# One more pair of k-tiles through sums in every second unit of the down product, and weight parts in whole chunks

## Chip, core and metric

The kernel runs on one core of one Trainium2 chip. The metric is the device time of one execution in microseconds. The core has a matrix engine (PE, with its weight loads shown as PEld), a vector engine (DVE), a scalar engine (ACT), a general engine (POOL) and a queue engine (SP) that issues most of the transfers. Each engine works through its own list of instructions.

## What is computed

Two layers of a decoder on 256 tokens of width 2048, all in float32. Each layer is a mixer and then a squared-ReLU MLP of width 8192. The parts that matter here:

```python
def channel_mlp(h, w_up, w_down):
    a = jax.nn.relu(h @ w_up)
    return (a * a) @ w_down
...
    for layer in range(DEPTH):
        ...
        h = rms_norm(x, ffn_norm[layer])
        x = x + channel_mlp(h, w_up[layer], w_down[layer])
```

`h @ w_up` is the up product (2048 to 8192), `(a * a) @ w_down` the down product (8192 to 2048).

## The kernel before

**Parts.** Every float32 operand of the big products is split into a high part (a copy on ACT into the reduced type `float32r`) and a low part (what is left, a subtraction on DVE). A product of two tiles is then three matmuls: high by high, high by low, low by high. Weights are streamed from memory and split as they come: a chunk is four k-tiles of 128 rows by 512 columns (1 MB), in one of three buffers `raw`. Its parts go to the pools `whi` and `wlo`. Before the change a buffer there holds two k-tiles (128x1024), and each pool has six of them; `load_chunk` (L57) makes two copies and two subtractions a chunk.

**Units.** In the up product and the mixers' products, `unit` and `unit_t` run over four chunks. In the products that end a mixer and in the down product, `wide` (L146) takes two column blocks of 512 and eight places; a place is a pair of k-tiles for both column blocks. It keeps four PSUM tiles `C[t][q]` (c00, c01, c10, c11: token half t, column block q), which ACT first fills with x (L151) and which DVE adds into x at the end (L217). A plain place makes eight products of three matmuls (24). A place in `sums` treats the 2x2 blocks (token halves by k-tiles, k-tiles by column blocks) with seven products (21 matmuls): sums of activations come ready from `combine` (tiles `combs`), sums of weights are made on DVE in the `raw` buffer (L175 to L178). Four of the seven results (1, 5, 7, 6) gather in PSUM tiles p1, p5, p7, p6 of their own. They are combined into s1, u2, u3 and w3 after the last place with sums (L197 to L201), at place 6.

**The down product.** `mlp` makes the up product in 16 blocks `up(j)` of 512 columns and the down product in four parts s. For each s, five blocks of `up` (four in the last) come first, then two units of `wide`: the first unit (`jw` = 0, output columns 0 to 1023) and the second unit (`jw` = 1, the rest). Both have sums at places 0, 2 and 4 of eight. So there are eight pairs of units in the two layers. At the end of layer 0, blocks of the next layer's input are turned (transposed on PE) from a list `pending`, one at place 6 and one at place 7 of the following unit, then one per chunk.

**Order.** A scheduler of the library orders the instructions of each engine when the program is built; every engine then takes its list in order and waits on semaphores. So instructions of several places can be interleaved, and the order changes with the code. The numbers behind tile names in the listings below are those of single buffers; they differ between the two programs.

Of the kernel before, what the change touches and what calls it, by code (L numbers as in the profile page):

```python
# [9 lines left out]
F32 = mybir.dt.float32  # L10
F32R = mybir.dt.float32r
# [5 lines left out]
P = 128  # L17
# [3 lines left out]
NB = 512  # L21
# [11 lines left out]
def trunk_kernel(ctx: ExitStack, tc, x, xT, vecs, sgu_gain, wsT, w_in, w_mix, w_qkv, w_ao, w_up, w_dn, out):  # L33
# [5 lines left out]
    parts = pool("parts", 6)  # L39
# [18 lines left out]
    def load_chunk(src, first=False):  # L58
# [3 lines left out]
        got = []  # L62
        for h in range(2):
            hi = parts.tile([P, 2, NB], F32R, name="whi")
            lo = parts.tile([P, 2, NB], F32R, name="wlo")
            for a, b in ((0, 1), (1, 2)) if first else ((0, 2),):
                w = raw[:, 2 * h + a:2 * h + b]
                nc.scalar.activation(hi[:, a:b], w, AF.Copy)  # L68
                nc.vector.tensor_tensor(lo[:, a:b], w, hi[:, a:b].bitcast(F32), ALU.subtract)  # L69
            got += [(hi[:, 0], lo[:, 0]), (hi[:, 1], lo[:, 1])]  # L70
# [50 lines left out]
    def combine(src):  # L121
# [8 lines left out]
        both = sums_of.tile([P, 2, 4, P], F32R, name="combs")  # L130
# [4 lines left out]
    def split_weights(w):  # L135

        n = w.shape[1]
        hi = parts.tile([P, 2, NB], F32R, name="whi")
        lo = parts.tile([P, 2, NB], F32R, name="wlo")
        nc.scalar.activation(hi[:, :n], w, AF.Copy)  # L140
        nc.vector.tensor_tensor(lo[:, :n], w, hi[:, :n].bitcast(F32), ALU.subtract)  # L141
        return hi, lo

    def wide(steps, src, x_of, sums=(0, 2, 4), last=False, behind=()):
# [14 lines left out]
        for n, (at, pair, i, comb) in enumerate(steps):  # L159
# [8 lines left out]
            cut = lambda both, q: tuple(w[:, q] for w in both)  # L168
            if n in sums:
# [3 lines left out]
                b11 = split_weights(left[:, 0:1])  # L173
                b2 = split_weights(raw[:, :, 1])
                nc.vector.tensor_tensor(left[:, 0], left[:, 0], right[:, 0], ALU.add)  # L175
                nc.vector.tensor_tensor(right[:, 0], right[:, 0], right[:, 1], ALU.add)  # L176
                nc.vector.tensor_tensor(right[:, 1], left[:, 0], right[:, 1], ALU.add)
                nc.vector.tensor_tensor(left[:, 1], right[:, 1], left[:, 1], ALU.add)  # L178
                t13 = split_weights(raw[:, :, 0])
                t42 = split_weights(raw[:, :, 1])  # L180
                if first:
                    mixed = {m: psum.tile([P, NB], F32, name=f"p{m}", tag="tp") for m in (1, 5, 7, 6)}
                for m in (1, 2, 3, 5, 7, 6, 4):
                    held, streamed = {
                        1: (a(0, 0), cut(b11, 0)), 2: (a(1, 0), cut(b2, 0)), 3: (s(3), cut(b2, 1)),
                        4: (a(1, 1), cut(t42, 0)), 5: (s(0), cut(t13, 0)), 6: (s(1), cut(t42, 1)),
                        7: (s(2), cut(t13, 1))}[m]
# [4 lines left out]
            else:  # L192
# [17 lines left out]
                for t, q, k in turns:  # L210
                    product(C[t][q], a(k, t), cut(both[k], q), False, n == 7 and k == 1)
# [465 lines left out]
```

## Time and profile before

| | |
|---|---|
| median of 3 runs | 2094.29 us (2094.15 to 2095.1) |
| the profiled execution | 2094.96 us, span 2093.2 us |
| PE busy | 2084.9 us, 100% of the span, 10300 matmuls |
| DVE busy | 1561.3 us, 75% |
| ACT busy | 1168.8 us, 56% |
| transfers | 403.39 MB, mean 193 GB/s |
| splitting weights, DVE | L69 519.1 us and L141 489.3 us |
| splitting weights, ACT | L68 454.2 us and L140 420.2 us |

A row of a group reads: line, engine, operation, output<-input, shapes, count, then busy time in us, mean of one in ns, and idle time ahead of it with what ended it. A row of the timeline or of the chain reads: start in us from the span's start, length in us, what, and how often in a row (x27); in brackets the idle time before it and its releaser. Matmuls are pipelined, so the mean of one in a group is longer than its share of a row of them.

### The profile page before, as it was taken

The numbers are of one execution on the slowest core, as the hardware profiler recorded it, in microseconds if no ns is written. First come the engines' busy times: TensorE is split into PE (matmuls) and PEld (weight loads), VectorE is DVE, ScalarE is ACT, GpSimd is POOL, SyncE is SP. The second block draws the span as 40 slices with busy tenths as digits, with TensorE's granted clock in tenths as the row PEclk, the third lists the DMA queues.
The fourth block names the chain that finished last, engine by engine and source line by source line (L and its number), as shares of the span: only waits on it lengthen the run. The fifth ranks groups of instructions, "written<-read, shape, count | busy, mean of one in ns | idle before, by whom it ended". The sixth has DMA issues, their size and how long they took to land.

```text
span 2093.2 us, 26935 instructions
## 1 busy us (share of the span) xinstructions
PE 2084.9 (100%) x10300; PEld 1763.4 (84%) x10300; DVE 1561.3 (75%) x2188; ACT 1168.8 (56%) x1556; POOL 3.8 (0%) x15
## 2 busy tenths in 40 slices
PE   9999999999999999999999999999999999999999
PEld 6888888888888888888888888888888888888887
DVE  6656887688678669678866667886696687688687
ACT  6544566655556465565554554765655555565554
POOL 0000000000000000000000000000000000000000
PEclk9999999999999999999999999999999999999999
DMA  8455465556546545645644444465456546546554
GB/s 342 181 201 181 161 219 187 182 184 218 194 159 224 207 161 198 222 160 201 220 175 178 168 159 167 161 223 183 163 197 222 200 163 239 184 157 235 190 186 156
DMA packets 81488, 403.39 MB, mean 193 GB/s; under 512 B 9168, under 2 KB 9936, under 8 KB 53840
## 3 DMA queue, kind: packets, MB, share of 16 engines
q1 hardware_dynamic: 80928, 401.25, 54.8%
q8 instruction: 80, 1.31, 0.2%
q10 hardware_dynamic: 432, 0.44, 0.1%
q14 instruction: 48, 0.39, 0.1%
HBM read 399.56 MB, written 2.10 MB: 192 GB/s over the span
## 4 chain that ended last, share of the span: by engine, by line
PE 99%; DMA 1%; DVE 0%; ACT 0%; DVEq 0%; issue 0%
PE c L156 32%; PE acc L95 23%; PE up L111 22%; PE up L116 12%; PE p L156 8%; PE tp L327 1%; PE tp L560 1%; PE tp L312 1%; DMA raw<-in_w_in 0%; PE tp L593 0%; PE tp L580 0%; PE tp L426 0%; PE tp L594 0%; DMA vec<-in_vecs 0%; PE tp L466 0%; DVE wlo L69 0%
## 5 line engine op out<-in xcount | busy, mean ns | idle before, releaser
L69 DVE TENSOR_TENSOR wlo<-raw,whi 128x1024 fp32r<-128x1024 f32 (+1 forms) x434 | 519.1, 1216 | 331.0 <-issue 193.4
L68 ACT ACTIVATE whi<-raw 128x1024 fp32r<-128x1024 f32 (+1 forms) x434 | 454.2, 1054 | 465.1 <-PE up L111 217.7
L140 ACT ACTIVATE whi<-raw 128x1024 fp32r<-128x1024 f32 (+1 forms) x440 | 420.2, 996 | 348.2 <-DVE raw L176 184.3
L156 PE MATMUL c<-whi,a 128*128 128x512 f32 x1840 | 588.3, 390 | 0.0
L141 DVE TENSOR_TENSOR wlo<-raw,whi 128x1024 fp32r<-128x1024 f32 (+1 forms) x440 | 489.3, 1147 | 112.7 <-ACT whi L140 58.7
L111 PE MATMUL up<-h,whi 128*128 128x512 f32 x2048 | 489.7, 391 | 0.0
L111 PEld LDWEIGHTS up<-h,whi 128*128 128x128 f32 x2048 | 376.6, 188 | 73.0
L156 PEld LDWEIGHTS c<-whi,a 128*128 128x128 f32 x1840 | 345.5, 188 | 72.2 <-ACT c L151 0.7
L95 PE MATMUL acc<-whi,h 128*128 128x512 f32 x1408 | 384.3, 391 | 2.6 <-ACT whi L68 2.0
L156 PE MATMUL c<-wlo,a 128*128 128x512 f32 x920 | 358.0, 389 | 0.0
L95 PEld LDWEIGHTS acc<-whi,h 128*128 128x128 f32 x1408 | 262.5, 188 | 57.7 <-ACT whi L68 3.3
L116 PEld LDWEIGHTS up<-h,wlo 128*128 128x128 f32 x2048 | 262.6, 191 | 10.0
L116 PE MATMUL up<-h,wlo 128*128 128x256 f32 x2048 | 265.7, 283 | 0.0
L95 PE MATMUL acc<-wlo,h 128*128 128x512 f32 x704 | 217.7, 390 | 0.5 <-DVE wlo L69 0.5
L156 PEld LDWEIGHTS c<-wlo,a 128*128 128x128 f32 x920 | 172.8, 188 | 35.7
L95 PEld LDWEIGHTS acc<-wlo,h 128*128 128x128 f32 x704 | 131.9, 188 | 29.2 <-DVE wlo L69 1.8
L156 PE MATMUL p<-whi,combs 128*128 128x512 f32 x360 | 120.7, 389 | 0.0
L156 PEld LDWEIGHTS p<-whi,combs 128*128 128x128 f32 x360 | 67.6, 188 | 13.8
L156 PE MATMUL p<-wlo,combs 128*128 128x512 f32 x180 | 70.8, 393 | 0.0
L217 DVE TENSOR_TENSOR x<-c,gc 128x512 f32<-128x512 f32 (+1 forms) x82 | 52.6, 670 | 17.0 <-PE c L156 16.9
L151 ACT ACTIVATE c<-x 128x512 f32<-128x512 f32 x80 | 45.7, 606 | 12.4 <-DVE x L217 12.2
L478 DVE TENSOR_TENSOR r<-up,r 128x256 f32<-128x256 f32 x128 | 47.8, 414 | 0.0
(127 smaller groups left out, 1185.1 us busy)
## 6 DMA issues: line engine op xcount, KB each, us to landing
raw<-in_w_up SPq DMA_DIRECT2D x128, 1024.0 KB, 4.8
raw<-in_w_dn SPq DMA_DIRECT2D x256, 512.0 KB, 4.9
raw<-in_w_qkv SPq DMA_DIRECT2D x48, 1024.0 KB, 4.8
raw<-in_w_in SPq DMA_DIRECT2D x39, 1024.0 KB, 4.8
raw<-in_w_mix SPq DMA_DIRECT2D x32, 512.0 KB, 4.9
raw<-in_w_ao SPq DMA_DIRECT2D x32, 512.0 KB, 4.8
x<-in_x SPq DMA_DIRECT2D x8, 256.0 KB, 7.3
xt<-in_xT SPq DMA_DIRECT2D x3, 512.0 KB, 10.3
```

What stands on the lines that cost most here:

```text
L68: nc.scalar.activation(hi[:, a:b], w, AF.Copy)
L69: nc.vector.tensor_tensor(lo[:, a:b], w, hi[:, a:b].bitcast(F32), ALU.subtract)
L95: nc.tensor.matmul(ps[t], held[:, k, t * P:(t + 1) * P], streamed, start=start, stop=stop)
L111: nc.tensor.matmul(ps[f], hi[:, f * P:(f + 1) * P], both[:, k], start=c == 0 and k == 0, stop=False, skip_group_check=True)
L116: nc.tensor.matmul(ps[f][:, 0], lo[:, f * P:(f + 1) * P], both[:, k, 0], start=False, stop=stop, skip_group_check=True)
L140: nc.scalar.activation(hi[:, :n], w, AF.Copy)
L141: nc.vector.tensor_tensor(lo[:, :n], w, hi[:, :n].bitcast(F32), ALU.subtract)
L151: nc.scalar.activation(C[t][q], x_of(t, q), AF.Copy)
L156: nc.tensor.matmul(ps, held[h], streamed[m], start=start and term == 0, stop=stop and term == 2, skip_group_check=True)
L217: nc.vector.tensor_tensor(xb, C[t][q][:, b:b + w], part[:, b:b + w], op)
L312: nc.tensor.transpose(tp[:, i * T + t * P:i * T + (t + 1) * P], x_sb[t][:, c:c + P], ident)
L478: nc.vector.tensor_tensor(r[:, f], ps[:, 0], r[:, f], ALU.add)
```

## The change

1. `sums` of the second unit becomes (0, 2, 4, 6), four places; the first unit takes its pairs in the order 1, 0, 3, 2, 5, 4, 6, 7 and has sums at places 1, 3, 5. The pairs with sums are 0, 2, 4 in the first unit, 0, 2, 4, 6 in the second. So `combine` is called for the first half of every block `up(j)`, and its fourth result for each s lies in a buffer of its own in the stage's pool.
2. s1, u2, u3, w3 are made at place `max(6, sums[-1] + 1)`: still 6 in the first unit, 7 in the second.
3. A buffer of weight parts holds four k-tiles; there are three instead of six. A chunk's low part is one subtraction of 128x2048, but for the very first chunk. In a place with sums, the four mixed weight tiles share one buffer and one such subtraction, and two of the four additions on weights become one of 2x512.

```diff
-    parts = pool("parts", 6)
+    parts = pool("parts", 3)
...
-        for h in range(2):
-            hi = parts.tile([P, 2, NB], F32R, name="whi")
-            lo = parts.tile([P, 2, NB], F32R, name="wlo")
-            for a, b in ((0, 1), (1, 2)) if first else ((0, 2),):
-                w = raw[:, 2 * h + a:2 * h + b]
-                nc.scalar.activation(hi[:, a:b], w, AF.Copy)
-                nc.vector.tensor_tensor(lo[:, a:b], w, hi[:, a:b].bitcast(F32), ALU.subtract)
+        hi = parts.tile([P, G, NB], F32R, name="whi")
+        lo = parts.tile([P, G, NB], F32R, name="wlo")
+        for a, b in ((0, 1), (1, 2), (2, 3), (3, 4)) if first else ((0, 2), (2, 4)):
+            nc.scalar.activation(hi[:, a:b], raw[:, a:b], AF.Copy)
+            if first:
+                nc.vector.tensor_tensor(lo[:, a:b], raw[:, a:b], hi[:, a:b].bitcast(F32), ALU.subtract)
+        if not first:
+            nc.vector.tensor_tensor(lo, raw, hi.bitcast(F32), ALU.subtract)
...
-        both = sums_of.tile([P, 2, 4, P], F32R, name="combs")
+        both = (home or sums_of).tile([P, 2, 4, P], F32R, name="combs", bufs=1 if home else 4)
...
+    def weight_parts():
+        return tuple(parts.tile([P, G, NB], F32R, name=name).rearrange("p (q k) n -> p q k n", q=2)
+                     for name in ("whi", "wlo"))
+    def split_weights(both, raw, *where):
+        for q, k in where:
+            nc.scalar.activation(both[0][:, q, k], raw[:, q, k], AF.Copy)
+        q, k = where[0] if len(where) == 1 else (slice(None), slice(None))
+        nc.vector.tensor_tensor(both[1][:, q, k], raw[:, q, k], both[0][:, q, k].bitcast(F32), ALU.subtract)
...
-                b11 = split_weights(left[:, 0:1])
-                b2 = split_weights(raw[:, :, 1])
-                nc.vector.tensor_tensor(left[:, 0], left[:, 0], right[:, 0], ALU.add)
-                nc.vector.tensor_tensor(right[:, 0], right[:, 0], right[:, 1], ALU.add)
+                split_weights(both, raw, (0, 0))
+                nc.scalar.activation(both[0][:, :, 1], raw[:, :, 1], AF.Copy)
+                nc.vector.tensor_tensor(both[1][:, :, 1], raw[:, :, 1], both[0][:, :, 1].bitcast(F32), ALU.subtract)
+                nc.vector.tensor_tensor(raw[:, :, 0], raw[:, :, 0], right, ALU.add)
                 nc.vector.tensor_tensor(right[:, 1], left[:, 0], right[:, 1], ALU.add)
                 nc.vector.tensor_tensor(left[:, 1], right[:, 1], left[:, 1], ALU.add)
-                t13 = split_weights(raw[:, :, 0])
-                t42 = split_weights(raw[:, :, 1])
+                mixed_w = weight_parts()
+                split_weights(mixed_w, raw, (every, 0), (every, 1))
...
-                both = [split_weights(raw[:, :, k]) for k in range(2)]
-                if n == 6:
+                split_weights(both, raw, (every, 0), (every, 1))
+                if n == max(6, sums[-1] + 1):
...
-                if 2 * (j % 4) + half in (0, 2, 4):
-                    combs[2 * j + half] = combine(r)
+                if half == 0:
+                    combs[2 * j] = combine(r, work if j % 4 == 3 else None)
...
+                order = range(8) if jw else (1, 0, 3, 2, 5, 4, 6, 7)
...
+                     sums=(0, 2, 4, 6) if jw else (1, 3, 5),
```

**At the start of the program, DVE.** `h` is the first activation, scaled and split; the last row of each listing is the low part of the second chunk. Before:

```order
L237 SCALAR_TENSOR_TENSOR h<-xt,vec,h 128x256
L69 TENSOR_TENSOR wlo<-raw,whi 128x512 x2
L237 SCALAR_TENSOR_TENSOR h<-xt,vec,h 128x256 x3
L237 SCALAR_TENSOR_TENSOR h<-xt,vec,h 128x256 x4
L69 TENSOR_TENSOR wlo<-raw,whi 128x1024 x2
```

And after:

```order
L243 SCALAR_TENSOR_TENSOR h<-xt,vec,h 128x256
L67 TENSOR_TENSOR wlo<-raw,whi 128x512 x2
L243 SCALAR_TENSOR_TENSOR h<-xt,vec,h 128x256 x3
L243 SCALAR_TENSOR_TENSOR h<-xt,vec,h 128x256 x4
L69 TENSOR_TENSOR wlo<-raw,whi 128x2048
```

The first chunk is unchanged; the second chunk's two subtractions are one.

**Where the first unit of the third pair of layer 0 passes into the second, DVE.** In the listing of before, c00_5072 to c11_5075 are the first unit's results, raw_5410 the weights of the second unit's first place, wlo_5426 and wlo_5430 the low parts of its sums of weights, and wlo_5462 that of the next place:

```order
L176 TENSOR_TENSOR raw_5410<-raw_5410 128x512
L177 TENSOR_TENSOR raw_5410<-raw_5410 128x512
L178 TENSOR_TENSOR raw_5410<-raw_5410 128x512
L141 TENSOR_TENSOR wlo_5426<-raw_5410,whi_5425 128x1024
L217 TENSOR_TENSOR x0_101<-c00_5072,gc_5332 128x512
L141 TENSOR_TENSOR wlo_5430<-raw_5410,whi_5429 128x1024
L217 TENSOR_TENSOR x0_101<-c01_5073,gc_5332 128x512
L217 TENSOR_TENSOR x1_102<-c10_5074,gc_5333 128x512
L217 TENSOR_TENSOR x1_102<-c11_5075,gc_5333 128x512
L141 TENSOR_TENSOR wlo_5462<-raw_5458,whi_5461 128x1024
```

After, c00_4735 to c11_4738, raw_5040, wlo_5053 and wlo_5086 are the same things:

```order
L207 TENSOR_TENSOR gc_4966<-p5_4793,gc_4966 128x512
L180 TENSOR_TENSOR wlo_5044<-raw_5040,whi_5043 128x2x512
L223 TENSOR_TENSOR x0_101<-c00_4735,gc_4965 128x512
L182 TENSOR_TENSOR raw_5040<-raw_5040 128x2x512
L223 TENSOR_TENSOR x0_101<-c01_4736,gc_4965 128x512
L183 TENSOR_TENSOR raw_5040<-raw_5040 128x512
L223 TENSOR_TENSOR x1_102<-c10_4737,gc_4966 128x512
L184 TENSOR_TENSOR raw_5040<-raw_5040 128x512
L223 TENSOR_TENSOR x1_102<-c11_4738,gc_4966 128x512
L145 TENSOR_TENSOR wlo_5053<-raw_5040,whi_5052 128x2048
L145 TENSOR_TENSOR wlo_5086<-raw_5082,whi_5085 128x2048
```

The additions on the weights stood ahead of all four additions into x and now stand between them; the low part of the sums of weights now comes behind all four.

**At the same place, ACT.** Before, whi_5425 and whi_5429 are the high parts of the first place's sums of weights, whi_5461 and whi_5465 the next place's, c00_5402 to c11_5405 the second unit's results being filled with x:

```order
L140 ACTIVATE whi_5413<-raw_5410 128x512
L140 ACTIVATE whi_5417<-raw_5410 128x1024
L140 ACTIVATE whi_5425<-raw_5410 128x1024
L140 ACTIVATE whi_5429<-raw_5410 128x1024
L151 ACTIVATE c00_5402<-x0_101 128x512
L151 ACTIVATE c01_5403<-x0_101 128x512
L140 ACTIVATE whi_5461<-raw_5458 128x1024
L151 ACTIVATE c10_5404<-x1_102 128x512
L151 ACTIVATE c11_5405<-x1_102 128x512
L140 ACTIVATE whi_5465<-raw_5458 128x1024
```

After, whi_5052 is the high part of the sums of weights (two copies), whi_5085 the next place's, whi_5117 that of the place behind it:

```order
L179 ACTIVATE whi_5043<-raw_5040 128x2x512
L154 ACTIVATE c00_5032<-x0_101 128x512
L143 ACTIVATE whi_5052<-raw_5040 128x2x512
L154 ACTIVATE c01_5033<-x0_101 128x512
L154 ACTIVATE c10_5034<-x1_102 128x512
L143 ACTIVATE whi_5085<-raw_5082 128x2x512
L154 ACTIVATE c11_5035<-x1_102 128x512
L143 ACTIVATE whi_5117<-raw_5114 128x512
```

Between c11_5035 and whi_5117 stand the second copies of whi_5052 and of whi_5085, in this order. The second copy of the sums' high part has moved from ahead of the four fillings to behind them.

**At the same place, PE.** Before, the second unit begins place by place:

```order
L156 MATMUL p1_5433<-whi_5413,a_3425 128x512
L156 MATMUL p1_5433<-wlo_5414,a_3425 128x512
L156 MATMUL c00_5402<-whi_5417,a_3425 128x512
L156 MATMUL c00_5402<-wlo_5418,a_3425 128x512
L156 MATMUL c01_5403<-whi_5417,combs_3612 128x512
L156 MATMUL c01_5403<-wlo_5418,combs_3612 128x512
L156 MATMUL p5_5434<-whi_5425,combs_3612 128x512
L156 MATMUL p5_5434<-wlo_5426,combs_3612 128x512
```

(of each product's three matmuls the third, which uses the high part again, is left out). After, the same nine matmuls into p1, c00 and c01 come first, and then:

```order
L159 MATMUL p5_5058<-whi_5052,combs_3375 128x512
L159 MATMUL p7_5059<-whi_5052,combs_3375 128x512
L159 MATMUL c00_5032<-whi_5085,a_3200 128x512
L159 MATMUL c01_5033<-whi_5085,a_3200 128x512
L159 MATMUL p6_5060<-whi_5052,combs_3375 128x512
L159 MATMUL c10_5034<-whi_5052,a_3200 128x512
L159 MATMUL c11_5035<-whi_5085,a_3200 128x512
L159 MATMUL p1_5057<-whi_5117,a_3987 128x512
L159 MATMUL p5_5058<-wlo_5053,combs_3375 128x512
```

Eight matmuls that need high parts alone, some of them of later places, have moved ahead of the first that needs wlo_5053.

More of the change, by code (lines that the diff above doesn't have):

```diff
@@ L61, in load_chunk @@
             nc.sync.dma_start(raw, src)
-        got = []
-        for h in range(2):
-            hi = parts.tile([P, 2, NB], F32R, name="whi")
-            lo = parts.tile([P, 2, NB], F32R, name="wlo")
-            for a, b in ((0, 1), (1, 2)) if first else ((0, 2),):
-                w = raw[:, 2 * h + a:2 * h + b]
-                nc.scalar.activation(hi[:, a:b], w, AF.Copy)
-                nc.vector.tensor_tensor(lo[:, a:b], w, hi[:, a:b].bitcast(F32), ALU.subtract)
-            got += [(hi[:, 0], lo[:, 0]), (hi[:, 1], lo[:, 1])]
+        hi = parts.tile([P, G, NB], F32R, name="whi")
[6 more added lines that the diff above has]
+            nc.vector.tensor_tensor(lo, raw, hi.bitcast(F32), ALU.subtract)
+        got = [(hi[:, k], lo[:, k]) for k in range(G)]
         return got
@@ L167, in wide @@
             a = lambda k, t: tuple(pair[:, 2 * i + k, m, t * P:(t + 1) * P] for m in range(2))
-            cut = lambda both, q: tuple(w[:, q] for w in both)
+            cut = lambda both, q, k: tuple(w[:, q, k] for w in both)
+            every = slice(None)
+            both = weight_parts()
             if n in sums:
@@ L210, in wide @@
                 for t, q, k in turns:
-                    product(C[t][q], a(k, t), cut(both[k], q), False, n == 7 and k == 1)
+                    product(C[t][q], a(k, t), cut(both, q, k), False, n == 7 and k == 1)
         for t, q, part, op in ((0, 0, s1, ALU.add), (0, 1, u2, ALU.add), (1, 0, u3, ALU.subtract), (1, 1, w3, ALU.add)):
@@ L498, in leave @@
                     nc.sync.dma_start(out[t * P:(t + 1) * P, at:at + xb.shape[-1]], xb)
-                wide([(n, lambda n=n: aT[4 * s + n // 2], n % 2, lambda n=n: combs.get(8 * s + n)) for n in range(8)],
+                order = range(8) if jw else (1, 0, 3, 2, 5, 4, 6, 7)
+                wide([(n, lambda n=n: aT[4 * s + n // 2], n % 2, lambda n=n: combs.get(8 * s + n)) for n in order],
                      [w_dn[layer, s, 2 * jw + q] for q in range(2)], lambda t, q: x_sb[t][:, cols(q)],
+                     sums=(0, 2, 4, 6) if jw else (1, 3, 5),
                      last=leave if s == 3 and gcol is None else False)
```

15 lines of the change are left out of this document (4 added, 11 removed).

## The prediction

> **What bounds the kernel.** I read the page first (busy times, the slices, the chain that ended last), then the chain in order of time over one pair of units of the down product, then the three engines there in order of time.
>
> ```profile
> span 2093.2 us, 26935 instructions
> PE 2084.9 (100%) x10300; PEld 1763.4 (84%) x10300; DVE 1561.3 (75%) x2188; ACT 1168.8 (56%) x1556; POOL 3.8 (0%) x15
> ...
> PEclk9999999999999999999999999999999999999999
> ...
> PE 99%; DMA 1%; DVE 0%; ACT 0%; DVEq 0%; issue 0%
> ```
>
> PE is busy throughout, at full clock, and 99% of the chain that ended last is PE. So a matmul taken away is worth what a matmul takes in a row of them, and a wait put on PE costs its full length.
>
> Next comes the chain for the third pair of units of layer 0 (start, length, what; p are the sums' products, c the plain ones), from the last piece of the stage before.
>
> ```profile
> 605.39 1.91 PE up L116 x16
> 607.31 0.69 PE p L156 x3
> ...
> 619.57 2.25 PE p L156 x9
> 621.82 6.15 PE c L156 x27
> ...
> 632.05 17.00 PE c L156 x75
> 649.05 0.68 PE p L156 x3
> ...
> 671.49 2.04 PE p L156 x9
> 673.53 17.00 PE c L156 x75
> 690.53 3.63 PE up L111 x16
> ```
>
> 75 matmuls in 17.00 us are 0.2267 us each; the mean of 390 ns in the groups counts the overlap and is no price. The first unit lasts from 607.31 to 649.05, the second to 690.53. With 183 matmuls each (3 x 21 + 5 x 24, 41.48 us) the second waits for nothing and the first loses 0.2 us, seen at 619.57: 2.25 where the same nine take 2.04 at 671.49. The busy time of the engines in these two stretches (in the order PE, PEld, DVE, ACT) shows how near the next limit is:
>
> ```profile
> 607.31:649.05 41.74, 41.74 (x184) 34.27 (x184) 39.73 (x54) 24.41 (x33) 0.00 (x0) 1.00 0.51 181
> 649.05:690.53 41.48, 41.48 (x185) 34.36 (x184) 35.33 (x40) 23.72 (x27) 0.00 (x0) 1.00 0.71 244
> ```
>
> DVE works 39.7 of 41.7 us in the first and 35.3 of 41.5 in the second: hidden here, but with little to spare, and the change gives the second unit more DVE work and less PE time.
>
> **Matmuls removed.** A place through sums has 21 matmuls, a plain one 24. Each of the eight second units (4 parts of each of 2 layers) gets one such place more: 24 matmuls, 24 x 0.2267 = **-5.4 us**. They lie on the path; there is no other bound for this term.
>
> **DVE and ACT work.** The durations of these forms:
>
> ```profile
> L141 DVE TENSOR_TENSOR wlo<-raw,whi 128x1024 fp32r<-128x1024 f32 x380 | 453.6, 1220 | 91.8 <-ACT whi L140 55.4 <-issue 22.3 <-PE up L116 10.8
> L141 DVE TENSOR_TENSOR wlo<-raw,whi 128x512 fp32r<-128x512 f32 x60 | 41.1, 685 | 20.9 <-issue 17.5 <-ACT whi L140 3.3
> L140 ACT ACTIVATE whi<-raw 128x1024 fp32r<-128x1024 f32 x380 | 389.0, 1054 | 335.3 <-DVE raw L176 184.3 <-DMA raw<-in_w_dn 50.8 <-PE up L111 35.8
> L151 ACT ACTIVATE c<-x 128x512 f32<-128x512 f32 x80 | 45.7, 606 | 12.4 <-DVE x L217 12.2
> L217 DVE TENSOR_TENSOR x<-c,gc 128x512 f32<-128x512 f32 x78 | 51.1, 683 | 16.1 <-PE c L156 15.9
> ```
>
> 512 more elements cost 1.220 - 0.685 = 0.535 us, so a subtraction of 128x2048, which the trace doesn't have, is put at 1.220 + 2 x 0.535 = 2.29 us. Its bounds are 2.14 (four times 0.535, no fixed part) and 2.44 (two of 1.22); I take 2.29, since the two rows give both the slope and the fixed part. Merging saves 2.44 - 2.29 = 0.15 us per pair merged, some 55 us of DVE time over 375 such instructions; eight more places with sums and eight more combinations spend about as much. DVE's total hardly moves; what counts is where it is late. ACT's work is the same but for eight copies of 0.6.
>
> **The start.** The second chunk's low part becomes one instruction for all four k-tiles and waits for both copies of ACT.
>
> ```profile
> 13.00 2.01 ACT L68 ACTIVATE whi<-raw 128x1024 fp32r<-128x1024 f32 x2 [0.94 <-DMA raw<-in_w_in]
> 14.09 2.36 DVE L69 TENSOR_TENSOR wlo<-raw,whi 128x1024 fp32r<-128x1024 f32 x2 [1.17 <-ACT whi L68]
> 15.37 0.73 PE L95 MATMUL acc<-wlo,h 128*128 128x512 f32 x2 [0.52 <-DVE wlo L69]
> ...
> 15.37 43.35 PE acc L95 x190
> ```
>
> Now DVE starts at 14.09, with the first half, and PE follows at 15.37. Then DVE starts at 13.00 + 2.01 + 0.02 = 15.03 and ends at 17.32: PE goes on at 17.37, and nothing later gives it back, since 190 matmuls follow without a gap. **+2.0 us**, between 1.8 and 2.1 with the bounds of the 128x2048.
>
> **Change from the first unit to the second**, eight times. The scheduler has put the additions on the weights of the second unit's first place between the four final additions into x, and one subtraction of 128x2048 behind them all. What stands there before:
>
> ```profile
> 642.76 0.68 DVE L175 TENSOR_TENSOR raw<-raw 128x512 f32<-128x512 f32 x1
> 643.48 0.69 DVE L176 TENSOR_TENSOR raw<-raw 128x512 f32<-128x512 f32 x1
> ...
> 646.68 0.68 DVE L217 TENSOR_TENSOR x<-c,gc 128x512 f32<-128x512 f32 x1
> 647.28 1.22 DVE L141 TENSOR_TENSOR wlo<-raw,whi 128x1024 fp32r<-128x1024 f32 x1
> 648.41 1.88 DVE L217 TENSOR_TENSOR x<-c,gc 128x512 f32<-128x512 f32 x3
> ...
> 647.39 0.60 ACT L151 ACTIVATE c<-x 128x512 f32<-128x512 f32 x1 [0.59 <-DVE x L217]
> 649.12 0.60 ACT L151 ACTIVATE c<-x 128x512 f32<-128x512 f32 x1 [1.13 <-DVE x L217]
> 649.66 1.04 ACT L140 ACTIVATE whi<-raw 128x1024 fp32r<-128x1024 f32 x1
> 650.61 1.10 ACT L151 ACTIVATE c<-x 128x512 f32<-128x512 f32 x2
> 651.65 2.52 ACT L140 ACTIVATE whi<-raw 128x1024 fp32r<-128x1024 f32 x3
> ```
>
> In a row, a DVE step of 512 takes 0.60 (646.68 to 647.28), one of 1024 1.13 (647.28 to 648.41); an ACT copy of 1024 takes 0.95 (649.66 to 650.61), one of c 0.52 (650.61 to 651.65, two). All weights of the first place were ready by 648.50, before PE came to them at 649.05. DVE comes to this point just in time: the first place's weights land 4.9 us after their buffer is free,
>
> ```profile
> raw<-in_w_dn SPq DMA_DIRECT2D x256, 512.0 KB, 4.9
> ```
>
> which by the same steps, summed from the unit's start, is 29.0 + 4.9 = 33.9 us into it; a copy of 512 (0.62) and DVE's 0.60, two combining steps of 0.60 and 1.13 follow, to 37.4, and c00's last matmul is the 165th, 165 x 0.2267 = 37.4. After, counted from that matmul: x from c00 0.04 later, then 0.60, the joint addition 1.13, x from c01 0.60, an addition 0.60, x from c10, which ends at 2.97 + 0.68 = 3.65. ACT, which waits for it, starts c10 at 3.68; behind it stand a copy of the next place at 4.20, c11 at 5.15 and only then the second copy of the first place's mixed weights, from 5.67 to 6.72. DVE subtracts from 6.75 to 9.04, PE may start at 9.08. PE gets there after 18 matmuls that end the first unit and 17 of the second that the scheduler moved ahead: 35 x 0.2267 = 7.93. It waits 1.15 us; the next subtraction (6.75 + 2.21 = 8.96, done 11.25) is needed nine matmuls on, at 11.12, and costs 0.15 more with the hop. So 1.3 us for each change of units, **+10.4 us**. Behind this DVE gains on PE: a place with sums and a plain one take it 0.60 + 1.13 + 1.25 + 0.72 + 1.78 + 2.21 + 2.21 = 9.9 us (the 1.78 is an addition, 0.69, and the copy it waits for, 1.05, with hops), PE 45 x 0.2267 = 10.2. Bounds: 0, as the row at 649.05 shows for the same place, and 2.1, if every step takes its mean and the subtraction 2.44 (9.9 + 0.15 against 7.93). I take 1.3: the rows are the same instructions in the same stage.
>
> The waits of 0.2 us at the first unit's third place go, since that place is plain: 8 x 0.2 = **-1.7 us** with the two slightly longer ones (0.2 to 0.4). The first unit itself, whose first place is now plain: it needs c10 after 16 matmuls (3.6 us).
>
> ```profile
> L478 DVE TENSOR_TENSOR r<-up,r 128x256 f32<-128x256 f32 x128 | 47.8, 414 | 0.0
> L236 ACT ACTIVATE h<-tp,vec 128x256 fp32r<-128x256 f32 x48 | 21.0, 471 | 20.8 <-DVE h L237 16.0 <-PE tp L312 4.7
> ```
>
> DVE first subtracts 128x2048 (from 607.46, when its buffer is free, to 609.7), then adds the stage before out of PSUM (0.41), then ACT writes c10 (0.61): 610.8, that is 3.5 us in. Nothing, within 0 to 0.2 each. At the end of layer 0 one block of the next layer's input is transposed a chunk later and used 6 matmuls (1.36 us) on; half its transposes and the first copy (0.47) fit into that: nothing. The coarser buffers elsewhere: a whole chunk (24 x 0.2267 = 5.4 us) lies ready ahead of PE, twice the 2.29 of the merged subtraction: nothing.
>
> A rule bears on the chain above. In the rows ACT ran 647.39, 649.12, 649.66, 650.61, 651.65 in just the program's order, idle 1.13 us ahead of the second. The Trainium skill, "TensorE: Matmul & The Clock Gate", section "Architectural detail: the array is 16× 32×32, not 1× 128×128", says that ScalarE and VectorE are strict first-in first-out and that only PE's weight loads may be pulled ahead; the trace agrees (idle 1.13 us), and no run here shows an overtaking. By that rule the sum is the one below; were a copy free to pass the waiting c11 and c10, the second mixed copy could start at 4.3 and the wait of 1.3 would be 0, as in the first rival.
>
> **Sum**: -5.4 + 2.0 + 10.4 - 1.7 = +5.3 us. The profiled execution took 2094.96 (span 2093.2), 0.7 over the median of 2094.29, so 2100.3 against 2094.96, or 2099.6 against the median.
>
> **Rivals.** *No wait at the change of units* (faster): the copies and the subtraction end within 7.93 us of c00's last matmul. For it: no wait there before, and matmuls that need only high parts have been moved ahead. Against: 9.08 by the steps. 2094.3 - 5.4 + 2.0 - 1.7 = 2089.2. It decides at 0.1 us a change; above, the gain falls below 0.2%. *Half the wait*, 0.65 us: 2094.4, no change; it holds if DVE or ACT steps run closer than in the rows, and spans waits of 0.15 to 1.15. *DVE falls behind for the whole second unit*: if the 128x2048 takes 2.44, the two places take 10.2, as long as PE, and no lateness is made good; 0.3 to 0.5 a unit more, 2103. Against: 9.9.
>
> **Numbers.** 0.2% (4.2 us) is about what a measurement of this kernel can tell from no change. Chances: wait of 1.15 or more, with the case that DVE falls behind, 0.45 (slower); half the wait 0.38 (same); none 0.17 (faster). Likeliest is the first, 2099.6, by itself 2098.5 to 2105. The range has to reach the other sign: 2089 to 2105.
>
> **What would show it.** PE 24 matmuls fewer; the gap ahead of the first wlo matmul of the second chunk about 2.5 us instead of 0.5; in each pair, at the second unit's first place, PE idle 1.0 to 1.5 us released by DVE wlo, with ACT's copies c10, whi, c11, whi in this order ahead; L145 at 128x2048 near 2.29. Wrong if the second units last 40.8 us (180 x 0.2267) with no wait, or if long waits stand in the middle of them.

## The result and the profile after

| | median, us | lowest to highest | runs |
|---|---|---|---|
| before | 2094.53 | 2094.15 to 2095.10 | 4 |
| after | 2117.91 | 2115.88 to 2118.07 | 4 |

The changed kernel is slower: ratio 1.011, 95% interval 1.0097 to 1.0122, that is +23.4 us. The forecast was 2099.6 (2089 to 2105): the sign was right, the size a quarter of what came, and the time lies outside the range. The profiled execution took 2118.07 us, its span is 23.1 us longer than before. Medians below leave out an execution over 1.5% slower than the fastest of its kernel, which one of experiment 11 was (4254.24 us).

The page after:

```profile
span 2116.3 us, 26341 instructions
PE 2096.8 (99%) x10276; PEld 1754.7 (83%) x10276; DVE 1573.1 (74%) x1833; ACT 1154.7 (55%) x1580; POOL 6.9 (0%) x15
...
PE 95%; DVE 3%; ACT 2%; DMA 1%; issue 0%; DVEq 0%; ACTq 0%
```

PE has the 24 matmuls fewer, and the chain that ended last now runs 5% of the time through DVE and ACT. PE's waits, the engine and line waited for, total us, times, longest:

```profile
PE p L159 <- ACT whi L143: 4.6, 8, 1.1
PE p L159 <- DVE wlo L145: 2.9, 8, 0.4
PE acc L95 <- DVE wlo L69: 2.5, 1, 2.5
PE c L159 <- DVE wlo L145: 1.9, 2, 0.9
```

Eight times two waits, one at the start, two more (these are in the two projections). They come to 12 us, and 28.5 have to be found: the 23.1 that the span grew and the 5.4 that the fewer matmuls should have saved. Two things hide the rest: the clock, and how a wait is counted, both below. The surest reading is the length of each stage, from its first matmul to the next stage's first, in PE's timeline (us; the last column is experiment 7, which has the new sums and no waits of PE behind the start):

| stage | before | after | exp. 7 |
|---|---|---|---|
| start to the first projection | 229.25 | 233.68 | 229.58 |
| first projection | 85.80 | 87.61 | 85.78 |
| the two up stages behind projections | 113.74, 113.76 | 113.86, 113.86 | 113.74, 113.74 |
| pairs of layer 0 | 83.18, 83.23, 83.18, 85.20 | 84.86, 85.09, 84.86, 87.23 | 82.54, 82.54, 82.54, 84.50 |
| attention's input and middle | 294.38 | 295.16 | 294.40 |
| second projection | 89.06 | 90.78 | 89.08 |
| pairs of layer 1 | 83.18, 83.18, 83.22, 82.98 | 84.83, 84.86, 84.90, 84.89 | 82.54, 82.54, 82.54, 82.54 |

The other up stages are equal (89.04, 66.77). So the pairs lost 14.2 us, the start 4.4, the projections 3.5, the border of the layers 0.8. The pair that the text so far calls the third of layer 0 is the second of its four pairs in this table (it is the third if the projection's is counted); it is called the second pair from here on. Now the places one by one.

**The start.** PE's timeline (start, length, instruction, idle ahead), then three lines of the chain around it, then the stretches 9.2 to 16.0, 16.0 to 22.8 and 22.8 to 29.6 us (busy time of PE, PEld, DVE, ACT, POOL; then the granted clock, the share of DMA, GB/s):

```profile
13.89 0.73 PE L95 MATMUL acc<-whi,h 128*128 128x512 f32 x2 [0.28 <-ACT whi L65]
17.17 1.22 PE L95 MATMUL acc<-wlo,h 128*128 128x512 f32 x2 [2.54 <-DVE wlo L69]
```
```profile
12.78 2.02 ACT whi L65 x2
...
14.82 2.30 DVE wlo L69
...
17.17 46.00 PE acc L95 x190
```
```profile
9.20:16.00 6.80, 5.15 (x20) 3.34 (x19) 5.13 (x10) 6.32 (x14) 0.00 (x0) 1.00 1.02 426
16.00:22.80 6.80, 5.63 (x13) 4.46 (x14) 6.80 (x11) 6.00 (x9) 0.00 (x0) 0.50 0.94 357
22.80:29.60 6.80, 6.80 (x31) 5.59 (x30) 4.18 (x2) 3.24 (x6) 0.00 (x0) 1.00 0.95 374
```

The gap is the one foretold, and PE goes on 1.80 us later than before (17.17 against 15.37). But the same 190 matmuls then take 46.00 us, not 43.35: the clock stands at 0.50 from 16.0 to 22.8, which costs 2.65 more.

**The change from first to second unit**, second pair of layer 0: PE, DVE, ACT.

```profile
660.77 0.63 PE L159 MATMUL c<-whi,a 128*128 128x512 f32 x2
661.90 0.51 PE L159 MATMUL p<-whi,a 128*128 128x512 f32 x1 [0.50 <-ACT whi L143]
662.76 0.50 PE L159 MATMUL p<-wlo,combs 128*128 128x512 f32 x1 [0.35 <-DVE wlo L145]
663.09 0.39 PE L159 MATMUL p<-whi,combs 128*128 128x512 f32 x1
663.33 0.39 PE L159 MATMUL p<-wlo,combs 128*128 128x512 f32 x1
```
```profile
653.66 0.69 DVE L223 TENSOR_TENSOR x<-c,gc 128x512 f32<-128x512 f32 x1 [0.41 <-PE c L159]
...
657.80 0.69 DVE L223 TENSOR_TENSOR x<-c,gc 128x512 f32<-128x512 f32 x1
660.41 5.09 DVE L145 TENSOR_TENSOR wlo<-raw,whi 128x2048 fp32r<-128x2048 f32 x3 [1.92 <-ACT whi L143]
```
```profile
657.33 0.60 ACT L154 ACTIVATE c<-x 128x512 f32<-128x512 f32 x1 [0.17 <-DVE x L223]
657.87 1.05 ACT L143 ACTIVATE whi<-raw 128x1024 fp32r<-128x1024 f32 x1
658.82 0.58 ACT L154 ACTIVATE c<-x 128x512 f32<-128x512 f32 x1
659.34 2.51 ACT L143 ACTIVATE whi<-raw 128x1024 fp32r<-128x1024 f32 x3
```

ACT does c10, a copy of the next place, c11, and then the second mixed copy, in the order foretold; DVE stands idle for 1.92 us ahead of the merged subtraction. PE's matmuls start 0.2267 us apart. After the two from 660.77 the next is due at 661.22 and comes at 661.90, 0.68 late; the one due at 662.13 comes at 662.76, 0.63 late; the next two follow at 663.09 and 663.33, the first of them 0.10 late. A further 0.05 and 0.11 are lost at the next subtraction, nine matmuls on: 1.57 us in all, where the idle times in brackets say 0.85.

**The first unit's first place.** The chain ahead of the same pair, which starts at 615.18:

```profile
609.77 3.67 PE up L111 x16
...
613.51 2.01 ACT whi L143 x2
615.52 0.28 ACT r L483
615.80 2.29 DVE wlo L145
618.09 0.35 DVE r L484
...
618.46 0.61 ACT c L154
...
619.12 4.15 PE c L159 x17
```

Sixteen matmuls after 615.18, at 618.84, PE wants c10; it comes at 619.12, and with the late matmul behind it this costs 0.39 us. This pair is the worst of the eight: the subtraction starts here at 615.80, 0.28 us after ACT's second copy has ended and right behind one of ACT's steps for the up stage (r), which it does not read; why it waits for that is open. In the other seven pairs it starts right behind the copy, c10 is there 3.64 us into the unit, and this place costs some 0.18 us. The next place, the one with sums, costs another 0.24 in each pair. Counted against experiment 7, the first units end 0.5 us late in seven pairs and 0.74 in this one, 4.3 us in all.

**The first projection.** PE and DVE at its change of units, where the place concerned is a plain one:

```profile
289.72 0.50 PE L159 MATMUL c<-wlo,a 128*128 128x512 f32 x1 [0.93 <-DVE wlo L145]
```
```profile
287.37 2.89 DVE L145 TENSOR_TENSOR wlo<-raw,whi 128x2048 fp32r<-128x2048 f32 x2 [1.90 <-ACT whi L143]
```

The same picture: DVE idle for 1.90 us, waiting for the second of two copies.

### The profile page after: what moved, and what is told of

It is laid out like the page before. It is cut to its first block, busy times and chain, and to the rows that moved or that the text cites. A ratio compares the mean times of both kernels' runs of the same rounds, so it can differ in the third digit from the quotient of the medians.

```text
span 2116.3 us, 26341 instructions
## 1 busy us (share of the span) xinstructions
PE 2096.8 (99%) x10276; PEld 1754.7 (83%) x10276; DVE 1573.1 (74%) x1833; ACT 1154.7 (55%) x1580; POOL 6.9 (0%) x15
## 4 chain that ended last, share of the span: by engine, by line
PE 95%; DVE 3%; ACT 2%; DMA 1%; issue 0%; DVEq 0%; ACTq 0%
PE c L159 28%; PE up L111 22%; PE acc L95 22%; PE up L116 11%; PE p L159 8%; DVE wlo L145 1%; ACT whi L143 1%; PE tp L333 1%; PE tp L318 1%; PE tp L569 0%; DMA raw<-in_w_in 0%; PE tp L602 0%; ACT junk L299 0%; ACT c L154 0%; PE tp L589 0%
## 5 line engine op out<-in xcount | busy, mean ns | idle before, releaser
L69 DVE TENSOR_TENSOR wlo<-raw,whi 128x2048 fp32r<-128x2048 f32 x215 | 492.1, 2291 | 303.0 <-ACT whi L65 301.2
L65 ACT ACTIVATE whi<-raw 128x1024 fp32r<-128x1024 f32 (+1 forms) x434 | 438.6, 1049 | 441.0 <-PE up L111 229.5
L159 PE MATMUL c<-whi,a 128*128 128x512 f32 x1744 | 566.5, 391 | 0.3 <-ACT whi L143 0.2
L143 ACT ACTIVATE whi<-raw 128x1024 fp32r<-128x1024 f32 (+1 forms) x388 | 362.6, 978 | 342.1 <-DVE raw L182 211.3
L145 DVE TENSOR_TENSOR wlo<-raw,whi 128x2048 fp32r<-128x2048 f32 (+1 forms) x228 | 404.5, 1811 | 131.8 <-ACT whi L143 103.3
L159 PEld LDWEIGHTS c<-whi,a 128*128 128x128 f32 x1744 | 327.3, 188 | 70.5 <-ACT c L154 2.9
L159 PE MATMUL c<-wlo,a 128*128 128x512 f32 x872 | 343.1, 393 | 1.9 <-DVE wlo L145 1.9
L159 PE MATMUL p<-whi,combs 128*128 128x512 f32 x408 | 139.2, 392 | 1.1 <-ACT whi L143 1.1
L182 DVE TENSOR_TENSOR raw<-raw 128x1024 f32<-128x1024 f32 x68 | 82.9, 1219 | 0.0
L180 DVE TENSOR_TENSOR wlo<-raw,whi 128x1024 fp32r<-128x1024 f32 x68 | 82.9, 1218 | 0.0
L179 ACT ACTIVATE whi<-raw 128x1024 fp32r<-128x1024 f32 x68 | 71.3, 1048 | 5.9 <-DMA raw<-in_w_dn 4.9
```

The costliest lines, as they stand in the source:

```text
L65: nc.scalar.activation(hi[:, a:b], raw[:, a:b], AF.Copy)
L69: nc.vector.tensor_tensor(lo, raw, hi.bitcast(F32), ALU.subtract)
L143: nc.scalar.activation(both[0][:, q, k], raw[:, q, k], AF.Copy)
L145: nc.vector.tensor_tensor(both[1][:, q, k], raw[:, q, k], both[0][:, q, k].bitcast(F32), ALU.subtract)
L159: nc.tensor.matmul(ps, held[h], streamed[m], start=start and term == 0, stop=stop and term == 2, skip_group_check=True)
L179: nc.scalar.activation(both[0][:, :, 1], raw[:, :, 1], AF.Copy)
```

## The experiments

Three theories were tried. Theory 1: merging two subtractions makes the low part wait for both of ACT's copies, and the second copy stands in ACT's queue behind work that is late; all waits come from this. Theory 2: the fourth pair through sums and the first unit's new order make DVE late. Theory 3: it is the coarser buffers. Experiments 1 to 4, 5 to 8, 9 to 11 and 12 are four groups, each run on one chip together with the kernel before, to which the ratios refer.

### 1. The new sums with the old parts

```diff
 # the kernel before, and from the change only:
-                if 2 * (j % 4) + half in (0, 2, 4):
+                if half == 0:
...
+                     sums=(0, 2, 4, 6) if jw else (1, 3, 5),
```

> The sums and their order as in the changed kernel, the weight parts, their subtractions and the additions as before (parts of two k-tiles, 128x1024). Theory 1, the merged subtraction of 128x2048 and the order that it brings make the waits: none is left, PE idles at no change of units and at no first place, the second chunk's gap is 0.5 us again; 2094.5 - 24 x 0.2267 = 2089.1, and 1 to 2 us less still where the 0.17 us waits of before at the first unit's third place go too. Theory 2, the fourth pair through sums and the first unit's new order make DVE late whatever the size of its instructions: about 1.6 us at each of eight changes of units and 0.6 at the first unit's first two places stay, 2089.1 + 8 x 2.2 = 2106.7.

2091.49 us, ratio 0.9985 (0.9976 to 0.9994). No wait of PE is left in any pair (82.54 to 82.58 us each but the last of layer 0, 83.55): theory 2 has fallen. It stays 2.4 us above the 2089.1 of theory 1; from layer 0's last pair to the second projection it takes 1.3 us more than before (380.85 against 379.58), where three matmuls fewer should have taken 0.7 less. Experiment 7 takes that up.

### 2. The coarse parts with the old sums

```diff
-                order = range(8) if jw else (1, 0, 3, 2, 5, 4, 6, 7)
+                order = range(8)
...
-                     sums=(0, 2, 4, 6) if jw else (1, 3, 5),
```

> The coarser parts, merged subtractions and additions of the changed kernel, with the sums and the orders of before (three pairs in each unit, k-tiles 0 to 7 in order; 24 matmuls are not removed). Theory 1: the start costs 1.8 (gap) + 2.65 (the slower stretch behind it), the two projections 1.8 each, the border of the layers 1.6, as in the changed kernel; the order of DVE at the change of units has all additions ahead of the final additions into x here, so that wait is at most a few tenths: 2094.5 + 9.7 = 2104, up to 2107. Theory 2: beside the start nothing, 2096 to 2099.

2126.50 us, ratio 1.0154 (1.0140 to 1.0168): worse than both, and 20 us more than I expected. Start (233.19) and projections (87.63, 90.80) are as in the changed kernel; the pairs, which I had put at nearly nothing, take 86.0 to 86.7 us, about 3 more than before (89.01 the last of layer 0, 3.8 more). PE in the second pair, which starts at 616.11:

```profile
631.01 0.49 PE L159 MATMUL p<-whi,a 128*128 128x512 f32 x1 [0.50 <-ACT whi L143]
631.87 0.50 PE L159 MATMUL p<-wlo,combs 128*128 128x512 f32 x1 [0.36 <-DVE wlo L145]
666.25 0.50 PE L159 MATMUL c<-wlo,a 128*128 128x512 f32 x1 [0.46 <-DVE wlo L145]
```
```profile
629.52 4.49 DVE L145 TENSOR_TENSOR wlo<-raw,whi 128x2048 fp32r<-128x2048 f32 x2 [1.15 <-ACT whi L143]
663.91 2.89 DVE L145 TENSOR_TENSOR wlo<-raw,whi 128x2048 fp32r<-128x2048 f32 x2 [2.44 <-ACT whi L143]
```

The second fence is DVE's merged subtractions ahead of these waits: at the first unit's third place, whose additions stand among the end of the up stage's work in DVE's queue, and at the change of units. All additions stand ahead of those into x at that change, as I had wanted, and the join is waited for all the same. So the coarse parts alone cost 32 us, and the new sums and orders save 5.4 of matmuls and 3 of waits.

### 3. Two subtractions for the second chunk

```diff
-            if first:
+            if first or halves:    # halves: the second chunk of the program
                 nc.vector.tensor_tensor(lo[:, a:b], raw[:, a:b], hi[:, a:b].bitcast(F32), ALU.subtract)
```

> The changed kernel, but the low part of the very second chunk of weights is made by two subtractions of 128x1024 instead of one of 128x2048; one more DVE instruction in all. Theory 1: the gap of 2.5 us ahead of its first wlo matmul goes back to about 0.5, and with it the stretch of halved clock from 16.0 to 22.8 us: 2117.9 - 1.8 - 2.65 = 2113.4. Rival: the halved clock has another cause than this gap (the load of the weights, the idle time ahead of it) and stays: 2116.

2113.26 us, 4.65 less than the changed kernel (ratio to before 1.0090, 1.0074 to 1.0106). The gap is back at 0.53 us, and so is the clock in the same stretch of time:

```profile
16.00:22.80 6.80, 6.80 (x30) 5.30 (x30) 6.10 (x11) 6.33 (x10) 0.00 (x0) 1.00 1.02 405
```

The start takes 230.00 us in its profile, 3.7 less than in the changed kernel. So one merged DVE instruction cost some 4 us: by the changed kernel's own rows 1.8 by the gap and 2.65 by the clock.

### 4. Halves everywhere, coarse buffers

```diff
         for q, k in where:
             nc.scalar.activation(both[0][:, q, k], raw[:, q, k], AF.Copy)
-        q, k = where[0] if len(where) == 1 else (slice(None), slice(None))
-        nc.vector.tensor_tensor(both[1][:, q, k], ...)
+            nc.vector.tensor_tensor(both[1][:, q, k], ...)
 # and the same in load_chunk
```

> The changed kernel with its buffers of four k-tiles and its joint additions, but every subtraction that makes low parts in two of 128x1024, one behind each copy. Theory 1 (the size of the instruction, and what it makes wait): start, projections and border as before, at the change of units the first half of the mixed low parts stands ahead of two of the final additions, so the wait is 0.5 us or less there: 2117.9 - 4.4 - 3.6 - 1.6 - 8 x 1.3 = 2098, down to 2090. Theory 3 (the buffers are released and filled four k-tiles at a time, and the instruction's size doesn't matter): 2110 or more, with ACT's copies waiting for PE.

2092.42 us, ratio 0.9989 (0.9980 to 0.9998). Buffers of four k-tiles and joint additions are kept, and 25.5 us are gone: theory 3 has fallen as the main cause, and what is left is the merged subtraction. The pairs take 82.53 to 82.59 (83.90 the last of layer 0).

### 5. Halves for the mixed weights alone

```diff
-                split_weights(mixed_w, raw, (every, 0), (every, 1))
+                for k in range(2):
+                    nc.scalar.activation(mixed_w[0][:, :, k], raw[:, :, k], AF.Copy)
+                    nc.vector.tensor_tensor(mixed_w[1][:, :, k], raw[:, :, k], mixed_w[0][:, :, k].bitcast(F32), ALU.subtract)
```

> The changed kernel, but only the low parts of the mixed weights (the places with sums) are made in two subtractions of 128x1024, one behind each copy; the plain places, the chunks and the buffers stay coarse. The additions on the second unit's first place still stand between the final additions into x, in the changed kernel's order. Theory 1a, the joint mixed subtraction alone makes the wait at the change of units: the first half stands ahead of the last addition into x and needs only the first copy, the second half is done about 7.9 us after c00's last matmul, when PE arrives; 8 x 1.4 to 1.6 us go, 2117.9 - 12 = 2106, while start, projections, border and first places stay. Theory 1b, the additions moved between those into x make ACT late whatever the subtraction: most of the wait stays, 2114 or more.

2102.26 us (ratio 1.0037, 1.0025 to 1.0050), 15.7 less than the changed kernel: as theory 1a had it, and more than its 12. The second pair takes 82.99; DVE at the change of units:

```profile
653.38 0.68 DVE L184 TENSOR_TENSOR raw<-raw 128x512 f32<-128x512 f32 x1
654.08 0.69 DVE L225 TENSOR_TENSOR x<-c,gc 128x512 f32<-128x512 f32 x1
654.69 1.22 DVE L188 TENSOR_TENSOR wlo<-raw,whi 128x1024 fp32r<-128x1024 f32 x1
655.83 0.68 DVE L225 TENSOR_TENSOR x<-c,gc 128x512 f32<-128x512 f32 x1
656.43 1.21 DVE L188 TENSOR_TENSOR wlo<-raw,whi 128x1024 fp32r<-128x1024 f32 x1
```

DVE has no idle time here. But the order changed in two more things: the joint addition on the weights (L182, at 650.45) now stands ahead of the first one into x (651.58), only the other two still between them, and ACT's second mixed copy stands ahead of c10's. So this run alone doesn't rule out 1b, and doesn't tell what it was; experiments 11 and 12 do.

### 6. PE kept busy in the gap

```diff
+                if first and n == 1 and k == 0 and term == 1 and t == 0:
+                    more = tps()
+                    for _ in range(10):
+                        nc.tensor.matmul(more, ahi[:, 0, :P], hi, start=True, stop=True)
```

> The changed kernel with ten matmuls more (128x512, into a PSUM tile that nothing reads) behind the two that need only the second chunk's first high part, so that PE is busy in most of the 2.5 us in which it waits for the low part. Theory 1: the clock is halved because PE stands idle there; with PE busy it stays at 1.00, the low part comes no sooner, and the time is 2117.9 - 2.65 = 2115.3, in every run. Rival: the clock falls for another reason (the load at the start), and the time stays 2117.9 in three runs of four.

2116.80 us (ratio 1.0107, 1.0092 to 1.0123). The low part comes no sooner, the idle time is 0.22 us, and the clock holds:

```profile
16.62 0.72 PE L99 MATMUL acc<-wlo,h 128*128 128x512 f32 x2 [0.22 <-DVE wlo L69]
```
```profile
15.50:22.30 6.80, 6.58 (x29) 5.09 (x29) 6.80 (x11) 5.97 (x9) 0.00 (x0) 1.00 0.95 349
```

The start is 2.9 us shorter in the profile (230.78 against 233.68). Of that the median shows only 1.1: the end of layer 0 took 1.0 more in this program (88.24 against 87.23, PE waits 0.80 us for x there), and one of the four executions had a mean clock of 0.999. The other three kept 1.000, where of the changed kernel's four only one did, under the same load of the start. So it is idle PE that lowers the clock; the gain in time is less than expected.

### 7. The turn taken at place 6

```diff
 # experiment 1, with the turn moved ahead of both branches for n >= 6:
             if n in sums:
+                if n >= 6 and pending:
+                    pending.pop(0)()
```

> The kernel of the first experiment (new sums, fine parts) with the transposes that wait their turn taken also at a place with sums from place 6 on; in the second units place 6 is now one, and without that the last block of layer 0 turns a chunk later. Theory 1: the waits at 1018 to 1050 us (2.0 us more than before, behind h's low parts and the first head norm) go, 2091.5 - 1.7 = 2089.8, about 5 us under the kernel before. Rival: these waits come from DVE's additional work for the fourth pair, not from the turn, and the time stays 2091.5.

2089.38 us, ratio 0.9975 (0.9966 to 0.9985): faster than the kernel before on the same chip (2094.70) by 5.3, about what the 24 matmuls are worth. It is the best kernel here. Last pair and attention together take 378.90 where experiment 1 took 380.85: the late turn had cost 2 us.

### 8. Four pairs through sums in both units

```diff
-                order = range(8) if jw else (1, 0, 3, 2, 5, 4, 6, 7)
+                order = range(8)
...
-                     sums=(0, 2, 4, 6) if jw else (1, 3, 5),
+                     sums=(0, 2, 4, 6),
```

> The kernel of the experiment with the earlier turn, with pairs 0, 2, 4, 6 through sums in both units, k-tiles in order: 192 matmuls fewer in the first units' eighth places (8 x 24 less 0), that is 8 x 3 x 8 = 24 x 1 for each unit, together 24 matmuls of 128x512 fewer than with the earlier turn. Theory: if DVE keeps up, 2089.8 - 5.4 = 2084.4. Against: DVE then has some 41 us of work in a first unit of 40.8, the four combining steps stand later and three of the additions on the next unit's first place come behind the additions into x, so that the change of units waits 1 us or more eight times: 2092 or more.

(What is fewer is 8 units x 3 matmuls = 24.) 2103.60 us, ratio 1.0041 (1.0028 to 1.0054). The pairs take 84.0 to 84.1 (88.10 the last of layer 0), 1.5 more than in experiment 7 in spite of 0.7 us fewer matmuls, with the waits at the change of units, as the second half of the expectation has it.

### 9. The same with a plain first place

```diff
-                order = range(8)
+                order = (1, 0, 3, 2, 5, 4, 6, 7)
...
+                     sums=(1, 3, 5, 6),
```

> The kernel of the earlier turn (fine parts) with four pairs through sums in both units, now at places 1, 3, 5, 6 with the k-tiles in the order 1, 0, 3, 2, 5, 4, 6, 7, so that each unit's first place is plain and no additions on weights stand at the change of units; 24 matmuls fewer than with the earlier turn. Theory: the wait of four sums in both units with the k-tiles in order (2.2 us a pair) came from the additions on the second unit's first place behind those into x; here it is gone, 2089.4 - 5.4 = 2084. Rival: DVE, with some 41 us of work in a unit of 40.8, is the bound whatever the order, and the last place's weights come late: 2092 or more.

2090.91 us, ratio 0.9982 (0.9973 to 0.9991): neither. The wait at the change is gone, but a pair takes 82.52 to 82.82 (84.70 the last of layer 0), as long as with 24 matmuls more. DVE's share points to a reason; the second pair, columns as above:

```profile
606.60:688.40 81.80, 81.80 (x359) 66.54 (x358) 79.17 (x100) 50.32 (x60) 0.00 (x0) 1.00 0.56 193
```

DVE works 79.2 of 81.8 us, and many matmuls start some hundredths late. I take DVE for the bound here; no run takes work off DVE to show it.

### 10. Halves everywhere, with the early turn

```diff
 # experiment 4, and the turn as in experiment 7
```

> The kernel with halves everywhere (coarse buffers and joint additions, subtractions of 128x1024), with the turn taken at place 6 too. If the border's loss is the late turn here as with fine parts: 2092.4 - 2.1 = 2090.3. If the coarse buffers have a cost of their own (1 us between the two kernels without the early turn), it stays: 2090.3 against 2089.4. Rival: with the early turn both are the same, 2089.4.

2090.74 us, ratio 0.9980 (0.9971 to 0.9989): 1.7 less than experiment 4. Last pair and attention take 378.38, 380.02 before: the turn works here too. Against experiment 7 it has 1.4 us more, of which its profile shows 0.5 in the two projections (86.09 and 89.27); a cost of the coarse buffers of this size is possible and wasn't tried further.

### 11. Halves cut the other way

```diff
+                for k in range(2):
+                    nc.scalar.activation(mixed_w[0][:, :, k], raw[:, :, k], AF.Copy)
+                for q in range(2):
+                    nc.vector.tensor_tensor(mixed_w[1][:, q], raw[:, q], mixed_w[0][:, q].bitcast(F32), ALU.subtract)
```

> The changed kernel, with the mixed low parts in two subtractions of 128x1024 as in the experiment on them, but cut the other way: each spans both k-tiles of one half of the columns, so that each needs both copies of ACT. It tells the size of the instruction from the wait for the second copy, which ACT makes behind c11's here, as in the changed kernel. Size alone: the wait at the change of units goes as with halves by k-tile, 2102 to 2104. Wait for the second copy alone: nothing is won, 2116 to 2118. Both: the first half is done 1.1 us sooner, PE then waits 0.7 us for the copy behind, 2117.9 - 8 x 0.8 = 2111.5.

2116.17 us (ratio 1.0100, 1.0084 to 1.0116): nearly as slow as the changed kernel, though each subtraction is a half. The pairs take 84.91 to 84.97 (87.47 the last of layer 0), as long as there (84.83 to 85.09, and 87.23). DVE and PE:

```profile
658.97 2.36 DVE L189 TENSOR_TENSOR wlo<-raw,whi 128x1024 fp32r<-128x1024 f32 x2 [1.92 <-ACT whi L187]
```
```profile
660.25 0.50 PE L159 MATMUL p<-wlo,combs 128*128 128x512 f32 x1 [0.28 <-DVE wlo L189]
663.59 0.50 PE L159 MATMUL c<-wlo,a 128*128 128x512 f32 x1 [0.73 <-DVE wlo L145]
```

DVE's 1.92 us of waiting for the second copy are there to a hundredth. The first half does come sooner for PE, but DVE is as late as before, and PE pays one place on (0.73 at 663.59). Size is not it. Nor is it the place of the joint addition, which stands ahead of the first one into x here as in experiment 5 (651.70 against 652.83): theory 1b falls for this addition, and in experiment 2, where all of them stand ahead, the join was waited for all the same.

### 12. One copy moved ahead in ACT's queue

```diff
-                split_weights(mixed_w, raw, (every, 0), (every, 1))
+                with tc.high_priority() if n == 0 else ExitStack():
+                    split_weights(mixed_w, raw, (every, 0), (every, 1))
```

> The changed kernel, with the scheduler's priority raised for the mixed copies and their joint subtraction at a second unit's first place. In the program's order this moves one thing at the change of units: ACT's second mixed copy stands ahead of c11's copy instead of behind it; DVE's order, the subtraction of 128x2048 and everything else there stay. Theory: the joint subtraction waits for ACT's second copy and for what is queued ahead of that; the copy ends 0.5 us sooner, the subtraction too, and PE's wait of 1.5 us becomes about 1.0: 2117.9 - 8 x 0.5 = 2113.9. Rival: PE's time there is set by the copy of the place after next (the 0.5 us wait for ACT ahead of it) or by DVE's length, and nothing is won: 2117 to 2118.

2112.01 us, 5.9 less than the changed kernel (ratio to before 1.0080, 1.0066 to 1.0094). DVE's order at this place is the changed kernel's, PE's differs by one matmul. From the first addition into x to the subtraction it is 6.22 us here, 6.75 in the changed kernel:

```profile
651.91 0.69 DVE L224 TENSOR_TENSOR x<-c,gc 128x512 f32<-128x512 f32 x1 [0.40 <-PE c L159]
...
658.13 5.10 DVE L145 TENSOR_TENSOR wlo<-raw,whi 128x2048 fp32r<-128x2048 f32 x3 [1.40 <-ACT whi L143]
```
```profile
660.14 0.49 PE L159 MATMUL p<-whi,a 128*128 128x512 f32 x1 [0.56 <-ACT whi L143]
```

0.53 us are what c11's copy takes in a row (0.52 in the changed kernel, 658.82 to 659.34). PE's wait for the subtraction is gone and that for ACT ahead of it stays (0.56): about half of the loss at this place is ACT's copy of a later place, as the rival had it. In the profiles the pairs have 4.6 us of the gain; 0.9 is the start, where the half clock lasted a shorter time in this execution. With the subtraction still joint, the place of one copy in ACT's queue moves the time: theory 1.

## Why the prediction was right or wrong

- *Matmuls, -5.4.* Right. A pair without waits takes 82.54 us, in most places 0.64 to 0.69 less than before, and experiment 7 is 5.3 us faster.
- *128x2048 at 2.29 us.* Right: 2.28 to 2.30 in all 375 of them, 2.29 in the mean.
- *Start, +2.0.* The gap was right (1.80). The step that failed is that nothing was to follow from it: PE's idle time brought 2.65 us by a halved clock, 4.4 in all. The Trainium skill, "TensorE: Matmul & The Clock Gate", section "What's actually happening", says that the clock goes to one half after an idle window of about 3.4 us, and that the window runs freely. By the length alone the trace differs: 2.54 us of idle were enough. The free window agrees: the half clock lasted 6.8 us, twice that window, and of the four executions one kept a mean clock of 1.000 and took 2115.88 us, the others 0.998 and 2117.8 to 2118.1.
- *Change of units, +10.4.* The mechanism, the order of ACT's copies and the times were right: the subtraction was to start 6.71 us after the first addition into x and started 6.75 after it. The size was 1.57 a change, not 1.3 (2.6 at the last pair of layer 0), 13.6 us in all: PE loses 0.1 more behind each wait, and it already waits for ACT's copy one step ahead. With the rule of the Trainium skill that the prediction named (strict first-in first-out on ScalarE) the trace agrees: in experiment 12 the copy came sooner by just what had stood ahead of it.
- *Third place, -1.7, and the first unit, nothing.* The wait at the third place went, but the first and second places took its room. The step that failed is the one for the first unit. DVE was to start its subtraction 0.15 us into the unit, on its own buffer alone. It started at 0.38 in seven pairs, since it also needs ACT's second copy (done at 0.34), and ACT could begin its copies only when PE's last high-part matmul had left the up stage (613.44 in the second pair, where DVE started at 0.62). c10 was there after 3.64 us, in that pair 3.89, not 3.5, and the second place, which had no term of its own, cost 0.24 more. That is 4.3 us in all.
- *Coarser buffers elsewhere, nothing.* Wrong by 3.5 us in the projections. I took a chunk of lead from the middle of the stages; at a change of units the lead is gone, since ACT has been busy with x, and the join then shows. With halves everywhere the projections lose only 0.3 us each (experiment 4: 86.09 and 89.33). The buffers themselves cost 1.4 us or so at most (experiments 7 and 10).
- *End of layer 0, nothing.* Wrong by 2 us (experiments 1 and 7, where the late turn is the only difference). I counted transposes and one copy, and not what stands behind them in DVE's queue; that it is this queue is my reading, and no run tests it.
- *DVE falls behind for the whole second unit* (a rival). Not so here; in experiment 9, with four pairs in both units, it seems to.

The common failure: I followed the join at the two places where I had seen it in the program's order, and gave every other merged subtraction a price of zero by its duration. What a merge costs is the wait for the last of its inputs, wherever the lead is short.

## What to carry to other kernels

Before two instructions are merged, ask when each input of the merged one comes, and from which place in a first-in first-out queue; the time saved on the instruction itself (0.15 us here) is small against a wait for the later input (1.9 us of DVE's time). Look for this at every change of stage, where the lead is short, not only where the edit was meant to work. When one change bundles a saving on the bounding engine with a merge elsewhere, time the two apart: here the first was worth -5 us and the second +32 (together +23, since the new order also takes away some waits).

## What the runs showed of the hardware

- *The clock falls for little idle time.* It went to one half for 6.8 us at a gap of 2.54 us, and in the middle of experiment 8 for 3.4 us behind one of 1.70 (PE's row, then the stretches around it). How long it lasts differs between executions: in the profiles of experiments 5, 2, 11 and 12, which have the same gap at the start, the half clock lasts 6.83, 3.41, 3.41 and 3.41 us. When stretches of 3.41 us are laid back to back from where the clock fell, those just ahead of a fall inside the program hold 1.53 to 2.54 us of idle PE, and one with 1.50 us, in experiment 2, was not followed by a fall; a length of gap alone doesn't tell.

```profile
976.52 0.73 PE L156 MATMUL p<-whi,combs 128*128 128x512 f32 x2 [1.70 <-ACT whi L140]
```
```profile
977.40:980.90 3.50, 3.43 (x8) 2.75 (x9) 3.50 (x4) 3.38 (x5) 0.00 (x0) 0.51 0.26 66
980.90:984.00 3.10, 3.10 (x15) 2.52 (x15) 3.07 (x5) 0.00 (x0) 0.00 (x0) 1.00 0.92 268
```

- *Idle time of PE understates a wait.* Each matmul is shown for 0.39 us, the next starts after 0.2267, so 0.16 us of every wait are covered, and short ones aren't seen at all; and the second matmul after a wait comes 0.1 late. At the change of units 0.85 us of idle time were 1.57 us of PE.
